# Rows of hx and g at places between the multiples of 32 bytes, and higher feature rates, in a one-core diffusion backbone step

## The chip, the cores and the metric

The kernel runs on one core of one Trainium2 chip. The metric is the device time of one execution in microseconds (us); smaller is better. Engines are named as in the profile: PE is TensorE (matmul), PEld its weight loads, DVE is VectorE, ACT is ScalarE, POOL is GpSimd, SP is SyncE, which issues the DMAs. Every operand of an engine lies in SBUF, 128 partitions wide; a "place" below is a byte address within each partition.

## What is computed

One step of a two-layer transformer for two groups of 128 tokens each (a context prompt and latent tokens), D_MODEL 2048. Both groups go through the same weights, so the kernel puts them side by side: 256 columns. Cut to what matters here:

```python
for l in range(2):
    mod = silu(cond) @ w_ada[l] + b_ada[l]            # six vectors of 2048 for each group
    sh1, sc1, gt1, sh2, sc2, gt2 = split(mod, 6)
    h = rmsnorm(x, g_norm_mix[l]) * (1 + sc1) + sh1   # "modulated"
    x = x + gt1 * mixer(h)                            # layer 0: MLA + GQA, layer 1: differential attention
    h = rmsnorm(x, g_norm_ffn[l]) * (1 + sc2) + sh2   # "modulated"
    u = conv3(h @ w_ffn_up[l])                        # 2048 -> 2 x 5632, then a depthwise convolution
    gate, val = u[..., :5632], u[..., 5632:]
    x = x + gt2 * ((silu(gate) * val) @ w_ffn_down[l])   # "gated"
y = rmsnorm(x, g_final)
```

All inputs and outputs are float32.

## The kernel before, in words

**Precision.** Every large product is made of three matmuls. `split` (L198 to L200) makes of a float32 operand a high part in the type fp32r (a copy by ACT) and the remainder, a low part (a subtraction by DVE). `gemm` (L238 to L248) then adds wh·xh, wh·xl and wl·xh for each block k of 128 input features: L245, L246, L247. The 128x128 block of weights is the loaded operand, the 256 columns of both groups are the moving operand. Weights come by DMA (1 MB each) into `raw` buffers and are split into `wh` and `wl` (`Weights.chunk`).

**Moving operands.** A row of one block k holds 512 numbers in each partition: 256 of the high part, 256 of the low part, 2048 bytes (`ROW` = 512 numbers). `hx` has 16 such rows; it holds the modulated activations (`modulate`, `modulated`, the first one in the main program), and in layer 0 also the attention's output (`o` in `mixer_ab`, under the same tag). `g` is the gated operand of the FFN's down-projection: 22 tiles of one row each (`bufs=KQ`), used twice, since the FFN runs in two halves of 22 blocks (NQ = 2). `oall`, `ql` and `kv_in` are the moving operands of other gemms.

**Places.** Tiles are put at multiples of 32 bytes. `pad` tiles (in `wpool`, `ab`, the FFN's pool and `cc`) move what follows them; SHIFT = 448. With them every row of hx, g, oall, ql and kv_in starts 448 bytes after the start of a weight buffer, modulo 512, which is the length of a 128-column block of weights in a partition. All hx and g rows are at 96, all weight blocks at 160, modulo 512.

**Stages.** Layer 0's mixer (`mixer_ab`, until about 470 us of the span), its FFN (about 490 to 1205), layer 1's mixer (`mixer_c`, to about 1650), the second FFN, and the final norm. An FFN is up(0), down(0), up(1), down(1): `up` has 44 gemms of 16 blocks for each half, `down` 16 gemms of 22 blocks.

**Side work.** The vectors `mod` need 2 x 2048 x 12288 weights (w_ada), which are read beside the gemms. `row_step` does units on PE (L338) or, for a few, on DVE (L367). `feature_step` does one on DVE (L323, one pass over a 128x2048 tile; eight steps make a unit, one DMA feeds two). `pump(rows, feats)`, called after each gemm, adds `feats` to a count and runs one feature step for each whole 1 in it. In the FFN `feats` is FRATE["up"] or FRATE["down"]; it is 0 for the first three blocks of `up` (LATE) and for the last four gemms of the last `down` (QUIET). What is left of the stage's units (13 in the first FFN, 15 by the end of the second: FLIMIT) runs after the last gemm, in the `while` at the end of `ffn`. A scheduler of the framework then orders the instructions of each engine; feature steps keep their order among DVE's pinned ones.

**After a stage.** The next one needs the norm of x: the sums of squares are multiplied out on PE (L179, L180), 1/sqrt on DVE and POOL (L170, L172), spread over partitions (L186 on DVE, L194 on PE), and `modulate` makes the rows of hx, block by block (L434, L440, L443, L444, L446).

Of the kernel before, what the change touches and what calls it, by code (L numbers as in the profile page):

```python
# [17 lines left out]
P = 128  # L18
D = 2048
KD = D // P  # L20
# [2 lines left out]
ROW = 2 * NT  # L23
SHIFT = 448
NL = 2
GRID_W = 64
EPS = 1e-6
MLA_SCALE = (128 + 64) ** -0.5
# [20 lines left out]
    _n += _w  # L49
NCONST = _n  # L50
RATE = {"in": 0.4, "in3": 0.25, "heads": 0.85, "out0": 1.2, "c": 0.65, "outc": 0.65}
FRATE = {"up": 0.735, "down": 1.435}
PEW = {"heads": 1.0, "out0": 1.0, "c": 0.5}
QUIET = [4, 3, 3]
LATE = 3
# [21 lines left out]
def step_kernel(ctx: ExitStack, tc: tile.TileContext, A: dict):  # L77
# [13 lines left out]
    def banks(name):  # L91
        return tc.tile_pool(name=name, bufs=1, space=PSUM)

    uid = [0]

    def nm(s):
# [3 lines left out]
    def T_(pl, shape, tag, dt=F32, bufs=None):  # L100
        kw = {} if bufs is None else {"bufs": bufs}
        return pl.tile(shape, dt, tag=tag, name=nm(tag), **kw)


    T_(wpool, [P, 48], "pad", bufs=1)


    cst = T_(keep, [P, NCONST], "cst")
# [340 lines left out]
    def modulated(st, l, which, units):  # L449
        ensure(l, 3 * which + 1)  # L450
        ensure(l, 3 * which)
        hx = T_(keep, [P, KD, ROW], "hx", F32R)
        modulate(hx, norm_scale(st), l, which, range(KD))
        fill(units)
        return hx
# [73 lines left out]
    def mixer_ab(hx, rb0, st):  # L529
        l = 0  # L530
        with tc.tile_pool(name="ab", bufs=1) as ab:
# [130 lines left out]
            with tc.tile_pool(name="abh", bufs=1) as hp:  # L662
                ada["pew"] = PEW["heads"]

                o = T_(keep, [P, KD, ROW], "hx", F32R)
                load_cw(0)
                WQ = Weights(A["w_q_up"], 6, 2)
                WK = Weights(A["w_kv_up"], 4, 4)
                qh, qlo = (lambda k: ql[:, k, :NT]), (lambda k: ql[:, k, NT:])
                kh, klo = (lambda k: kv_in[:, k, 0]), (lambda k: kv_in[:, k, 1])  # L670
                qn, qr = {}, None

                def gqa_query(h):
                    s2 = T_(tmp, [P, NT], "sq", bufs=2)
                    act.activation(s2, qb[:, h], AF.Square)
                    act.activation(qb[:, h], qb[:, h], AF.Identity, scale=C("gqn"))
                    yield
                    pst = T_(pmisc, [P, 512], "misc")
                    for g in range(2):
                        pe.matmul(pst[:, g:g + 1], s2[:, g * T:(g + 1) * T], inv(128),  # L680
                                  start=True, stop=True)
                    r = rstd(pst[:, 0:2], 2)
                    pool.tensor_scalar(out=rsb[:, h], in0=r[:, 0:2], scalar1=HEAD_SCALE,
                                       scalar2=None, op0=ALU.mult)
                    rope(qb[:, h:h + 1, T:], qb[:, h:h + 1, T:], 1, 64, "rch", "rsh")

                def gqa(h):
                    k = kg[:, h // 4]
                    return head_ab(hp, [(qb[:, h], k)], rsb[:, h], lambda b: vg[:, b, h // 4], o, 8 + h)

                def mla(h, qnh, qrh, knh, vh):
                    half = slice(64 * (h % 2), 64 * (h % 2) + 64)
                    return head_ab(hp, [(qnh, knh), (qrh[half], kr[half])], rsm,
                                   lambda b: vh[:, b], o, h)

                flush()
                start(gqa_query(0))
                for h in range(8):
                    if h % 2 == 0:
                        for i in range(2):  # L700
                            ps = gemm(WQ.chunk(), qh, qlo)
                            qn[h + i] = T_(hp, [P, NT], "qn", bufs=4)
                            act.copy(qn[h + i], ps)
                            pump(RATE["heads"])
                        ps = gemm(WQ.chunk(), qh, qlo)
                        ev = T_(tmp, [P, NT], "nt", bufs=4)
                        act.copy(ev, ps)
                        qr = T_(hp, [P, NT], "qr", bufs=2)
                        act.copy(qr[:, 0:T], ev[:, 0:T])
                        rope(qr[:, None, T:], ev[:, None, T:], 1, 32, "rcm", "rsm")  # L710
                        pump(RATE["heads"])
                    if h < 7:
                        start(gqa_query(h + 1))
                    start(gqa(h))
                    ps = gemm(WK.chunk(), kh, klo, 3 * T)
                    kn = T_(hp, [P, 3 * T], "kn", bufs=2)
                    act.copy(kn, ps)
                    pump(RATE["heads"])
                    ps = gemm(WK.chunk(), kh, klo, 3 * T)
                    vt = T_(hp, [P, 3 * T], "vt", bufs=2)  # L720
                    act.copy(vt, ps)
                    pump(RATE["heads"])

                    def values_and_head(h, vt, *a):
                        pt = T_(ppool["att"], [P, 512], "att", bufs=3)
                        for b in range(3):
                            pe.transpose(pt[:, b * T:(b + 1) * T], vt[:, b * T:(b + 1) * T], ident)
                        vm = T_(hp, [P, 3, P], "vm", bufs=2)
                        act.copy(vm.rearrange("p b d -> p (b d)"), pt[:, :3 * T])
                        yield  # L730
                        yield from mla(h, *a, vm)

                    start(values_and_head(h, vt, qn[h], qr, kn))
                flush()
# [129 lines left out]
    def ffn(hx, l, st):  # L864
        xh, xl = (lambda k: hx[:, k, :NT]), (lambda k: hx[:, k, NT:2 * NT])
        W = Weights(A["w_up"][l], KD, 1)
        WD = Weights(A["w_down"][l], KQ, TB)
        cw = ada["cw"]
        with tc.tile_pool(name=f"ffn{l}", bufs=1) as fp, banks(f"pffn{l}") as pf:
            feat["home"], feat["pool"] = fp, pf  # L870
            T_(fp, [P, SHIFT // 4], "pad")

            def conv(ps, m):
                y = T_(fp, [P, NT], "cv", bufs=3)
                act.activation(y, ps, AF.Identity, scale=cw[:, 1, m:m + 1], bias=cw[:, 3, m:m + 1])  # L875
                y3 = y.rearrange("p (g t) -> p g t", g=2)
                p3 = ps.rearrange("p (g t) -> p g t", g=2)
                dve.scalar_tensor_tensor(out=y3[:, :, 1:], in0=p3[:, :, :T - 1],  # L878
                                         scalar=cw[:, 0, m:m + 1], in1=y3[:, :, 1:],
                                         op0=ALU.mult, op1=ALU.add)  # L880
                dve.scalar_tensor_tensor(out=y3[:, :, :T - 1], in0=p3[:, :, 1:],  # L881
                                         scalar=cw[:, 2, m:m + 1], in1=y3[:, :, :T - 1],
                                         op0=ALU.mult, op1=ALU.add)
                return y

            def up(q):
                gs = []
                for i in range(q * KQ, (q + 1) * KQ):
                    rate = 0 if i < LATE else FRATE["up"]
                    fine[0] = False  # L890
                    gate = conv(gemm(W.chunk(), xh, xl), i)
                    pump(0, rate)
                    if i == 0:
                        load_row()
                    val = conv(gemm(W.chunk(), xh, xl), NFF + i)
                    pump(0, rate)
                    act.activation(gate, gate, AF.Silu)
                    dve.tensor_tensor(out=val, in0=gate, in1=val, op=ALU.mult)
                    g = T_(fp, [P, ROW], "g", F32R, bufs=KQ)
                    split(g[:, :NT], g[:, NT:2 * NT], val)  # L900
                    gs.append(g)
                return gs

            def down(gs, q):
                for c in range(KD):
                    quiet = q == NQ - 1 and c >= KD - QUIET[0]
                    fine[0] = quiet
                    ps = gemm(WD.chunk(), lambda k: gs[k][:, :NT], lambda k: gs[k][:, NT:2 * NT])
                    residual(ps, l, 1, c, st if q == NQ - 1 else None)
                    pump(0, 0 if quiet else FRATE["down"])  # L910

            for q in range(NQ):
                gs = up(q)
                if q == 0:
                    ensure(l, 5)
                down(gs, q)
            while feat["i"] < FLIMIT[stage[0]]:
                feature_step()


    with banks("pab") as ppool["ada"]:
# [5 lines left out]
        st = stat_init()  # L927
        for c in range(KD):
            stat_add(st, x[:, c], KD)
        hx = T_(keep, [P, KD, ROW], "hx", F32R)  # L930
        rb0 = norm_scale(st)
        st = stat_init()
        mixer_ab(hx, rb0, st)
# [150 lines left out]
```

## Time and profile before

| | us |
|---|---|
| Time, median of 3 runs | 2401.15 |
| Lowest, highest | 2400.2, 2407.49 |
| Profiled execution, its time | 2405.92 |
| Profiled execution, its span (first to last instruction) | 2404.2 |
| DVE busy in the span | 1764.9 |
| ACT busy in the span | 1161.7 |
| Moved by DMA | 612.92 MB, 255 GB/s |

How to read it: a page of the profile gives busy times by engine, the granted clock of PE in 40 slices, the chain of work that ended last, and groups of instructions by source line, with the mean duration of one and the idle time before them. A matmul's duration is a latency, because matmuls overlap; its cost in a row of them is the distance between two starts, which the timeline shows.

### The profile page before, as it was taken

Reading aid. Unit: us, or ns where it says so; the run is one execution under the profiler, and the core shown is the slowest. Engines: PE = TensorE matmul, PEld = TensorE weight load, DVE = VectorE, ACT = ScalarE, POOL = GpSimd, SP = SyncE. Lnnn points to the kernel's source line nnn. Section 1 sums busy time; section 2 is a strip of 40 time slices with the busy share of each in tenths; the row PEclk is TensorE's granted clock in tenths of the full one; section 3 lists DMA queues with packets and bytes.
Section 4 is the critical chain, followed back from the end, with each engine's and each line's share of the span. In section 5 each row is a group of like instructions: output and inputs, shape, how many; then the busy total and the mean of one; then the engine's idle time right before and its main releaser. Section 6 shows DMA issues by size and latency. Waiting matters only on the chain.

```text
span 2404.2 us, 47304 instructions
## 1 busy us (share of the span) xinstructions
PE 2329.8 (97%) x19664; PEld 2190.5 (91%) x19664; DVE 1764.9 (73%) x2699; ACT 1161.7 (48%) x1815; POOL 176.3 (7%) x211
## 2 busy tenths in 40 slices
PE   6999999999999999999989999999999999999997
PEld 3778868799999999999969999987999999999997
DVE  2467534579999999999879797876898655666654
ACT  4336544455554355554445454445555534555542
POOL 2002101100000000001210001022000000000011
PEclk9999999999999999999989999999999999999999
DMA  9886678867777877777776777856775555555553
GB/s 394 319 322 245 232 271 311 331 249 266 263 267 284 294 287 263 263 261 278 288 290 230 288 266 275 293 214 249 270 267 198 193 193 193 194 193 193 193 193 123
DMA packets 92549, 612.92 MB, mean 255 GB/s; under 512 B 9968, under 2 KB 17840, under 8 KB 20400
## 3 DMA queue, kind: packets, MB, share of 16 engines
q1 hardware_dynamic: 92336, 609.91, 69.3%
q8 instruction: 154, 2.52, 0.4%
q14 instruction: 59, 0.48, 0.1%
HBM read 605.12 MB, written 4.75 MB: 254 GB/s over the span
## 4 chain that ended last, share of the span: by engine, by line
PE 92%; DMA 4%; DVE 2%; issue 1%; ACT 1%; POOL 0%; POOLq 0%; SPq 0%; DVEq 0%; ACTq 0%
PE acc L245 28%; PE acc L246 28%; PE acc L247 28%; PE ada L338 4%; DMA araw<-w_ada 2%; PE att L509 1%; DMA ckc<-cache_ckv 1%; DMA raw<-w_in_ab 0%; PE ada L286 0%; PE att L801 0%; PE att L499 0%; DMA raw<-w_ada 0%; DMA condb<-condb 0%; DVE nt L440 0%; DVE x L953 0%
## 5 line engine op out<-in xcount | busy, mean ns | idle before, releaser
L199 ACT CAST wh<-raw 128x1024 fp32r<-128x1024 f32 (+1 forms) x788 | 794.4, 1013 | 1007.9 <-PE acc L246 855.7
L200 DVE TENSOR_TENSOR wl<-raw,wh 128x1024 fp32r<-128x1024 f32 (+1 forms) x788 | 921.6, 1182 | 410.3 <-ACT wh L199 402.6
L245 PE MATMUL acc<-hx,wh 128*128 128x256 f32 x4208 | 1170.8, 280 | 12.0 <-ACT hx L444 11.4
L246 PE MATMUL acc<-hx,wh 128*128 128x256 f32 x4208 | 1170.2, 279 | 0.4 <-DVE hx L446 0.4
L247 PE MATMUL acc<-hx,wl 128*128 128x256 f32 x4208 | 1169.0, 278 | 0.0
L245 PEld LDWEIGHTS acc<-hx,wh 128*128 128x128 f32 x4208 | 791.3, 189 | 48.1 <-ACT hx L444 19.4
L246 PEld LDWEIGHTS acc<-hx,wh 128*128 128x128 f32 x4208 | 792.9, 189 | 21.2 <-issue 16.5
L247 PEld LDWEIGHTS acc<-hx,wl 128*128 128x128 f32 x4208 | 792.6, 188 | 13.8 <-issue 13.7
L246 PE MATMUL acc<-g,wh 128*128 128x256 f32 x1408 | 388.3, 276 | 0.0
L247 PE MATMUL acc<-g,wl 128*128 128x256 f32 x1408 | 388.1, 276 | 0.0
L245 PE MATMUL acc<-g,wh 128*128 128x256 f32 x1408 | 387.9, 276 | 0.0
L323 DVE CUSTOM_DVE_ANT_0 junk<-araw,condb 128x2048 f32<-128x2048 f32 x120 | 274.6, 2288 | 0.0
L246 PEld LDWEIGHTS acc<-g,wh 128*128 128x128 f32 x1408 | 264.3, 188 | 0.0
L247 PEld LDWEIGHTS acc<-g,wl 128*128 128x128 f32 x1408 | 264.2, 188 | 0.0
L245 PEld LDWEIGHTS acc<-g,wh 128*128 128x128 f32 x1408 | 264.1, 188 | 0.0
L165 POOL TENSOR_TENSOR sqacc<-sqacc,sq 128x256 f32<-128x256 f32 x76 | 92.9, 1222 | 1530.5 <-issue 1221.2
L338 PE MATMUL ada<-araw,condw 128*32 128x512 f32 x864 | 121.3, 635 | 22.7 <-DMA araw<-w_ada 17.2
L367 DVE SCALAR_TENSOR_TENSOR aacc<-araw,condw,aacc 128x512 f32<-128x512 f32 x150 | 107.7, 747 | 0.3
L875 ACT ACTIVATE cv<-acc,convw 128x256 f32<-128x256 f32 x176 | 98.1, 557 | 0.0
L460 DVE SCALAR_TENSOR_TENSOR x<-acc,mod,x 128x128 f32<-128x128 f32 x192 | 58.1, 344 | 53.4 <-PE acc L247 53.4
L881 DVE SCALAR_TENSOR_TENSOR cv<-acc,convw,cv 128x254 f32<-128x254 f32 x176 | 84.2, 479 | 3.9
L878 DVE SCALAR_TENSOR_TENSOR cv<-acc,convw,cv 128x254 f32<-128x254 f32 x176 | 83.4, 474 | 0.0
(195 smaller groups left out, 1623.3 us busy)
## 6 DMA issues: line engine op xcount, KB each, us to landing
araw<-w_ada SPq DMA_DIRECT2D x188, 1024.0 KB, 5.7
raw<-w_up SPq DMA_DIRECT2D x176, 1024.0 KB, 4.8
raw<-w_down SPq DMA_DIRECT2D x88, 1024.0 KB, 4.8
raw<-w_in_c SPq DMA_DIRECT2D x48, 1024.0 KB, 5.1
raw<-w_in_ab SPq DMA_DIRECT2D x20, 1024.0 KB, 6.9
raw<-w_out_ab SPq DMA_DIRECT2D x16, 1024.0 KB, 6.3
raw<-w_out_c SPq DMA_DIRECT2D x16, 1024.0 KB, 4.9
raw<-w_q_up SPq DMA_DIRECT2D x6, 768.0 KB, 4.6
```

What stands on the lines that cost most here:

```text
L165: pool.tensor_tensor(out=st["acc"], in0=st["acc"], in1=sq, op=ALU.add)
L199: act.copy(out_hi, src)
L200: dve.tensor_tensor(out=out_lo, in0=src, in1=out_hi.bitcast(F32), op=ALU.subtract)
L245: pe.matmul(ps[:, :n], wh, xh(k), start=(i == 0), stop=False)
L246: pe.matmul(ps[:, :n], wh, xl(k), start=False, stop=False)
L247: pe.matmul(ps[:, :n], wl, xh(k), start=False, stop=(i == last))
L323: tc.keep_in_program_order(dve.tensor_tensor_reduce(out=T_(feat["pool"], [P, D], "junk"), in1=feat["row"][:, c], in0=feat["raw"].rearrange ...
L338: i = pe.matmul(ada["ps"][32 * g:32 * g + 32, :], condw[:, 4 * t + g, :], raw[:, g], start=(t == 0), stop=(t == 3), skip_group_check=True)
L367: i = dve.scalar_tensor_tensor(out=acc[:, c], in0=raw[:, g], scalar=condw[:, k, c:c + 1], in1=acc[:, c], op0=ALU.mult, op1=ALU.add)
L875: act.activation(y, ps, AF.Identity, scale=cw[:, 1, m:m + 1], bias=cw[:, 3, m:m + 1])
L878: dve.scalar_tensor_tensor(out=y3[:, :, 1:], in0=p3[:, :, :T - 1], scalar=cw[:, 0, m:m + 1], in1=y3[:, :, 1:], op0=ALU.mult, op1=ALU.add)
L881: dve.scalar_tensor_tensor(out=y3[:, :, :T - 1], in0=p3[:, :, 1:], scalar=cw[:, 2, m:m + 1], in1=y3[:, :, :T - 1], op0=ALU.mult, op1=ALU.add)
```

## The change

Two tables give each row of hx and of g an offset of its own, in numbers of 4 bytes: HX_AT for the 16 rows of hx is 0, 2, 4, 6 by groups of four; G_AT for the 22 rows of g is 4, 4, ... (six times), 6 (six), 9 (five), 11 (five). A small class `Rows` stands for such a tile: `rows[:, k, a:b]` is the slice from ROW * k + at[k] + a. hx grows by 8 numbers (32 bytes), and the pad in `wpool` shrinks by as much, so that the weight buffers stay where they were. g becomes one tile of 22 rows and 16 numbers for each FFN, in place of 22 tiles; it now stands right behind the pad, which is 8 numbers (32 bytes) shorter, and the tiles `cv` and `condb` come after it. oall, ql and kv_in stay.

FRATE goes from 0.735 to 0.75 in `up` and from 1.435 to 1.47 in `down`.

```diff
+
+HX_AT = [2 * (k // 4) for k in range(16)]
+G_AT = [4] * 6 + [6] * 6 + [9] * 5 + [11] * 5
...
-FRATE = {"up": 0.735, "down": 1.435}
+FRATE = {"up": 0.75, "down": 1.47}
...
+    class Rows:
+
+
+        def __init__(self, tile_, at):
+            self.tile_, self.at = tile_, at
+
+        def __getitem__(self, key):
+            _, c, s = key
+            a = ROW * c + self.at[c]
+            return self.tile_[:, a + (s.start or 0):a + s.stop]
...
-    T_(wpool, [P, 48], "pad", bufs=1)
+    T_(wpool, [P, 40], "pad", bufs=1)
...
-        hx = T_(keep, [P, KD, ROW], "hx", F32R)
+        hx = Rows(T_(keep, [P, KD * ROW + 8], "hx", F32R), HX_AT)
         modulate(hx, norm_scale(st), l, which, range(KD))
...
-                o = T_(keep, [P, KD, ROW], "hx", F32R)
+                o = Rows(T_(keep, [P, KD * ROW + 8], "hx", F32R), HX_AT)
...
-            T_(fp, [P, SHIFT // 4], "pad")
+            T_(fp, [P, SHIFT // 4 - 8], "pad")
+            rows = Rows(T_(fp, [P, KQ * ROW + 16], "g", F32R), G_AT)
...
-                    g = T_(fp, [P, ROW], "g", F32R, bufs=KQ)
-                    split(g[:, :NT], g[:, NT:2 * NT], val)
-                    gs.append(g)
+                    k = i - q * KQ
+                    split(rows[:, k, :NT], rows[:, k, NT:2 * NT], val)
+                    gs.append((rows[:, k, :NT], rows[:, k, NT:2 * NT]))
...
-                    ps = gemm(WD.chunk(), lambda k: gs[k][:, :NT], lambda k: gs[k][:, NT:2 * NT])
+                    ps = gemm(WD.chunk(), lambda k: gs[k][0], lambda k: gs[k][1])
...
-        hx = T_(keep, [P, KD, ROW], "hx", F32R)
+        hx = Rows(T_(keep, [P, KD * ROW + 8], "hx", F32R), HX_AT)
         rb0 = norm_scale(st)
```

## The prediction

> **What bounds the kernel now.** I read the page first, engines and slices, then the chain of waits.
>
> ```profile
> span 2404.2 us, 47304 instructions
> PE 2329.8 (97%) x19664; PEld 2190.5 (91%) x19664; DVE 1764.9 (73%) x2699; ACT 1161.7 (48%) x1815; POOL 176.3 (7%) x211
> PEclk9999999999999999999989999999999999999999
> PE 92%; DMA 4%; DVE 2%; issue 1%; ACT 1%; POOL 0%; POOLq 0%; SPq 0%; DVEq 0%; ACTq 0%
> ```
>
> TensorE (PE) is busy 97% of the span at full granted clock, and 92% of the chain that ended last is PE. So the time is a count of matmuls times what one of them takes, plus some stops at the stage borders. Next the groups of instructions, for the counts:
>
> ```profile
> L245 PE MATMUL acc<-hx,wh 128*128 128x256 f32 x4208 | 1170.8, 280 | 12.0 <-ACT hx L444 11.4
> L246 PE MATMUL acc<-hx,wh 128*128 128x256 f32 x4208 | 1170.2, 279 | 0.4 <-DVE hx L446 0.4
> L247 PE MATMUL acc<-hx,wl 128*128 128x256 f32 x4208 | 1169.0, 278 | 0.0
> L245 PE MATMUL acc<-g,wh 128*128 128x256 f32 x1408 | 387.9, 276 | 0.0
> L286 PE MATMUL ada<-cst,am 128*128 128x128 f32 x122 | 19.4, 279 | 4.4 <-ACT am L280 4.4
> ```
>
> 3 x 4208 = 12,624 matmuls stream rows of hx and 3 x 1408 = 4,224 rows of g. Their mean of 276 to 280 ns is a latency, since matmuls overlap; what one costs is the distance from start to start. That is read from the timeline. The first two rows are six matmuls apart, the next two eighteen; the last is four matmuls of 128 columns in one row.
>
> ```profile
> 699.80 0.28 PE L247 MATMUL acc<-hx,wl 128*128 128x256 f32 x1
> 700.48 0.28 PE L247 MATMUL acc<-hx,wl 128*128 128x256 f32 x1
> ...
> 1579.81 0.28 PE L246 MATMUL acc<-oall,wh 128*128 128x256 f32 x1
> 1581.93 0.28 PE L246 MATMUL acc<-oall,wh 128*128 128x256 f32 x1
> ...
> 1237.49 0.60 PE L286 MATMUL ada<-cst,am 128*128 128x128 f32 x4
> ```
>
> 0.68 / 6 = 113.3 ns, and 2.12 / 18 = 117.8 ns: two rhythms of one instruction form, with the same weight load and the same distance (448 bytes modulo 512) between moving row and weight buffer. The fast one is the rule:
>
> ```profile
> 600.00:900.00 300.00, 300.00 (x2650) 300.00 (x2649) 280.00 (x347) 142.43 (x177) 0.00 (x0) 1.00 0.76 278
> 1045.00:1160.00 115.00, 115.00 (x1017) 115.00 (x1016) 109.59 (x127) 53.87 (x68) 16.20 (x8) 1.00 0.77 279
> 1595.00:1640.00 45.00, 45.00 (x384) 45.00 (x384) 24.73 (x37) 19.54 (x31) 10.24 (x8) 1.00 0.53 188
> 1880.00:1990.00 110.00, 110.00 (x973) 110.00 (x972) 64.37 (x83) 47.35 (x54) 0.00 (x0) 1.00 0.55 192
> ```
>
> These windows (length; then busy time and count of PE, weight loads, DVE, ACT, POOL; clock; DMA) lie in the first ConvFFN, twice, in the output projection of layer 1, and in the second ConvFFN. 300 / 2650 = 113.2 ns in the first row, 113.1 in the second and the last, whether DVE is at 95% (109.59 of 115) or at 59%, and DMA at 0.77 or 0.55. The third has 117.2, with less beside it than any other. So in 113.3 ns there is no wait for another engine: it is what the array and its two streams of operands do by themselves. A lower bound for the pair of weight load and matmul comes from the L286 row: four matmuls, each with a 128x128 load, take 0.60 us, less one latency of 279 ns: 107 ns. So at most about 6 ns of each 113 is an extra that depends on something else.
>
> [...]
>
> **The change, part by part.**
>
> *Places.* HX_AT puts rows 0 to 3 of hx where they were, and rows 4 to 7, 8 to 11, 12 to 15 at 8, 16, 24 bytes further. G_AT is 16, 24, 36, 44 bytes, and the pad ahead of g is 32 bytes shorter: so g's rows move by -16 (six rows), -8 (six), +4 (five), +12 bytes (five). Pads keep every weight buffer, and oall, ql and kv_in, where they were. No instruction is added or removed: 12,624 x 3/4 = 9,468 matmuls on hx and all 4,224 on g, 13,692 in all, read from another place. What that is worth no row shows directly, since every gemm of this trace has the one distance. So I bound it.
> Best: each moved matmul falls to the 107 of L286: 13,692 x 6.3 ns = 86 us. Worst that a row shows: each goes to the other rhythm: 13,692 x 4.5 = 62 us more.
> My value: 1,024 bytes of a row go by in 113.3 ns, so 8 bytes are 0.89 ns. [...] I let each move take its own length off the extra. hx: moves of 0, 8, 16, 24 bytes, mean 12, 1.33 ns x 12,624 = 16.8 us. g: (6x16 + 6x8 + 5x4 + 5x12) / 22 = 10.2 bytes, 1.13 ns x 4,224 = 4.8 us. Together 21.6 us, a quarter of the best case, since all moves lie within 28 bytes of a 512-byte distance. That the sign is a gain is the weakest step; it is weighed below.
>
> *Writers.* ACT and DVE write these rows in instructions of 0.4 us; they are under PE in the FFN, and on the chain only at the start of a stage. If the places cost each of them what 16 bytes of 1,024 are, 6 ns, 16 rows x 3 stages x 2 writers come to 0.6 us. I take nothing.
> *g as one tile.* Before, 22 buffers were reused by the second half of the FFN; now 22 slices are. Each write waits for the reads of its own slice, as before: nothing.
>
> *Rates.* In the first FFN 104 feature steps are due. pump counts 0.735 on 82 calls and 1.435 on 28: 60.3 + 40.2 = 100.5, so 100 run inside and 4 after the last gemm. With 0.75 and 1.47 it is 61.5 + 41.2 = 102.7: 102 inside, 2 after. What the four do now, by DVE's timeline, then PE's:
>
> ```profile
> 1205.88 2.29 DVE L323 CUSTOM_DVE_ANT_0 junk<-araw,condb 128x2048 f32<-128x2048 f32 x1
> 1209.22 0.15 DVE L170 TENSOR_SCALAR rv<-misc 128x2 f32<-128x2 f32 x1
> 1209.29 2.29 DVE L323 CUSTOM_DVE_ANT_0 junk<-araw,condb 128x2048 f32<-128x2048 f32 x1
> 1212.17 0.48 DVE L186 TENSOR_SCALAR diag<-cst,rr 128x128 f32<-128x128 f32 x2 [0.53 <-POOL rr L172]
> 1212.56 2.29 DVE L323 CUSTOM_DVE_ANT_0 junk<-araw,condb 128x2048 f32<-128x2048 f32 x1
> 1214.78 1.41 DVE L434 TENSOR_TENSOR nt<-x,misc 128x256 f32<-128x256 f32 x4
> 1216.10 2.29 DVE L323 CUSTOM_DVE_ANT_0 junk<-araw,condb 128x2048 f32<-128x2048 f32 x1
> 1218.31 1.11 DVE L440 TENSOR_SCALAR nt<-nt,scl,mod 128x128 f32<-128x128 f32 x4
> ...
> 1212.80 1.19 PE L194 MATMUL misc<-diag,cst 128*128 128x256 f32 x2 [4.98 <-DVE diag L186]
> 1218.51 1.94 PE L338 MATMUL ada<-araw,condw 128*32 128x512 f32 x8 [4.52 <-DVE mod L323]
> 1220.37 0.80 PE L245 MATMUL acc<-hx,wh 128*128 128x256 f32 x2
> ```
>
> The third and the fourth step stand in the way of the norm that the first gemm of layer 1 waits for. In the changed order they are the two that leave. Without the third, L434 can begin when L194 ends (1212.80 + 1.19 = 1213.99 instead of 1214.78): 0.8 us. Without the fourth, L440 follows L434 directly: 2.2 us. Gain 3.0 us; at most 4.6 (two steps of 2.29), at least 0, if the row steps L338 are what is late next. The two steps go under PE into the first FFN, whose tightest window above leaves DVE 115 - 109.59 = 5.4 us; were that cover gone they would cost their 4.6 us. One more 1 MB load there meets DMA at 0.77. In the second FFN the 16 steps only end sooner.
>
> *Sum.* The profiled execution took 2405.9 us, 1.7 beside its span. 2405.9 - 21.6 - 3.0 = 2381.3. It lies 4.8 us over the median of the runs (2401.15), so the median goes to about 2377.
>
> **The rivals.**
> (a) *The places do nothing.* For it: the rhythm is the same for hx and g, and with busy and idle neighbours, as a fixed cost would be. Against it: 117.8 at the same places shows a cost that isn't fixed. Only the tail is left: 2401.2 - 3.0 = 2398. [...]
> (b) *A row that starts inside a 16-byte piece touches one piece more, and the result is slower.* A row of 1,024 bytes is 64 pieces of 16; at a start off that grid it touches 65. Rows at +8 and +24 of hx (half of 12,624) and at -8, +4, +12 of g (16 of 22 of 4,224) are such: 6,312 + 3,072 = 9,384 matmuls x 113.3 / 64 = 1.77 ns: 16.6 us, less 3.0: 2415. It decides where the extra piece isn't hidden in the 6 ns over L286; nothing in this trace starts off that grid, so no row speaks against it. [...]
> (c) *The moves push gemms into the slow rhythm.* 117.8 exists, and holds for whole stretches, as in the 45 us window of the output projection; that stage follows attention, whose short matmuls cut into the gemms. A jump of place three times in each gemm might do the same. In full 62 us, less 3: 2460; with half of the rows 2429. Against it: hx and g keep the fast rhythm through both FFNs undisturbed.
> [...]
>
> **How the numbers follow.** A measurement here can't tell less than about 0.3%, 7 us, from no change. Forecast 0.48; (a) 0.15; (b) 0.17; (c) 0.15; (d) 0.05. I put the forecast ahead of (b) and (c) because g's moves go to both sides of the old place and all four groups differ: what costs at one place is then bounded by the others, while the fast rhythm that holds across every neighbour's load speaks against (c). The forecast alone reaches from 2350 (twice the value) to 2392 (a third of it). To leave out no more than 2 in 10, the range takes in (a), (b) and the half of (c), and below all but the end of (d): 2341 to 2430. Faster by over 0.3%: the forecast and (d), less the forecast's small end: 0.50. Within 0.3%: (a) and that end: 0.17. Slower: (b), (c): 0.33.
>
> **What would show it.** Start-to-start distances of the hx and g matmuls: near 112 ns in the FFN windows, about 2,680 matmuls in 300 us instead of 2,650, and steps by group of rows in the timeline. Rows of oall stay at 117.8 or 113.3. The first gemm of layer 1 follows L194 by about 4.6 us instead of 7.6, with two L323 steps between the last L460 and L434 instead of three, and none after it. Wrong if the distance is still 113.3 (a), if the rows at +8 and +24 alone are longer (b), if long stretches of an FFN run at 117 and over (c), or if PE gets idle time behind wl in the first FFN, since then DVE has become the bound.

## The result, and the profile after

| | before | after |
|---|---|---|
| Time, median, us | 2402.2 (4 runs) | 2486.3 (4 runs) |
| Ratio of after to before, 95% interval | | 1.0338, 1.0322 to 1.0354 |
| Span of the profiled execution, us | 2404.2 | 2479.8 |

The change makes the kernel 3.4% slower; the prediction had 2377 us and a range of 2341 to 2430. The page of the profile after, in the lines that were read before:

```profile
span 2479.8 us, 47330 instructions
PE 2411.2 (97%) x19664; PEld 2272.5 (92%) x19664; DVE 1764.2 (71%) x2699; ACT 1157.3 (47%) x1815; POOL 168.1 (7%) x211
PE 94%; DMA 3%; DVE 1%; issue 1%; ACT 1%; POOL 0%; SPq 0%; POOLq 0%; DVEq 0%; ACTq 0%
L259 PE MATMUL acc<-hx,wh 128*128 128x256 f32 x4208 | 1192.2, 285 | 11.4 <-ACT hx L458 10.5
L259 PE MATMUL acc<-g,wh 128*128 128x256 f32 x1408 | 396.7, 282 | 0.0
```

PE is busy 81 us longer with the same 19,664 matmuls; DVE and ACT have the same work in the same time; PE still hardly waits (11.4 us in front of 4,208 matmuls of L259, where it was 12.0 at L245, the same line of the code). So no new wait: the matmuls themselves take longer. The windows show it. Rows of PE alone (length; busy time and count; clock; DMA share; GB/s), first of before, then of after; the first of each pair is an `up` stretch, that is hx alone, the second a `down` stretch, g alone. A count holds two matmuls that began ahead of the window. Only the moving rows of hx and g, which lie in SBUF like the weights, have new places; the sums `acc` are in PSUM and did not move.

```profile
920.00:1020.00 100.00, 100.00 (x885) 1.00 0.74 269
2002.00:2024.00 22.00, 22.00 (x197) 1.00 0.56 194
```

```profile
920.00:1020.00 100.00, 100.00 (x846) 1.00 0.70 259
2002.00:2024.00 22.00, 22.00 (x186) 1.00 0.51 176
```

100 / 883 = 113.3 ns has become 100 / 844 = 118.5 on hx, and 22 / 195 = 112.8 has become 22 / 184 = 119.6 on g; the clock is 1.00 in all four. Added up over all starts of the two traces, matmuls on hx take 1477.1 us before and 1533.7 after (+56.6), on g 478.7 and 504.8 (+26.1), on oall, which was not moved, 94.5 and 91.3 (-3.2), everything else on PE 3.6 less. The sum is 75.9 us, against 75.6 between the two spans.

Which rows pay is seen inside one gemm. Below are single starts of a gemm of `up` in the trace after: of its matmuls number 0, 4, 12, 24, 36, and number 0 of the next gemm. Three matmuls belong to a row, so 12, 24 and 36 are the first ones at +8, +16 and +24 bytes.

```profile
903.61 0.28 PE L259 MATMUL acc<-hx,wh 128*128 128x256 f32 x1
904.08 0.28 PE L260 MATMUL acc<-hx,wh 128*128 128x256 f32 x1
904.99 0.28 PE L259 MATMUL acc<-hx,wh 128*128 128x256 f32 x1
906.43 0.28 PE L259 MATMUL acc<-hx,wh 128*128 128x256 f32 x1
907.86 0.28 PE L259 MATMUL acc<-hx,wh 128*128 128x256 f32 x1
909.30 0.28 PE L259 MATMUL acc<-hx,wh 128*128 128x256 f32 x1
```

From 4 to 12, in the rows that stayed: 0.91 / 8 = 114 ns. At +8: 1.44 / 12 = 120; at +16: 1.43 / 12 = 119; at +24: 1.44 / 12 = 120. Even the rows that stayed pay once: their first four matmuls, after the last rows of the gemm before, take 0.47 / 4 = 118. So each group of moved rows is slower than the rows at the old place in this gemm, and the slowdown ends within four matmuls when the place is the old one again.

The means over the distances between two starts of the same group of rows, interruptions over 128 ns left out, in ns:

```
bytes moved        -16    -8     0     +4    +8   +12   +16   +24
hx (after)                      115.2        120.1       118.9  120.4
g  (after)        118.9  119.7        121.4        118.1
```

### The profile page after: what moved, and what is told of

It reads as the page before. It is cut to its first block, busy times and chain, and to the rows that moved or that the text cites. A ratio compares the mean times of both kernels' runs of the same rounds, so it can differ in the third digit from the quotient of the medians.

```text
span 2479.8 us, 47330 instructions
## 1 busy us (share of the span) xinstructions
PE 2411.2 (97%) x19664; PEld 2272.5 (92%) x19664; DVE 1764.2 (71%) x2699; ACT 1157.3 (47%) x1815; POOL 168.1 (7%) x211
## 4 chain that ended last, share of the span: by engine, by line
PE 94%; DMA 3%; DVE 1%; issue 1%; ACT 1%; POOL 0%; SPq 0%; POOLq 0%; DVEq 0%; ACTq 0%
PE acc L259 29%; PE acc L261 29%; PE acc L260 29%; PE ada L352 4%; DMA araw<-w_ada 1%; PE att L523 1%; DMA ckc<-cache_ckv 1%; PE ada L300 0%; DMA raw<-w_in_ab 0%; PE att L815 0%; DMA raw<-w_ada 0%; PE att L513 0%; DMA condb<-condb 0%; DVE x L968 0%; PE ada L287 0%
## 5 line engine op out<-in xcount | busy, mean ns | idle before, releaser
L259 PE MATMUL acc<-hx,wh 128*128 128x256 f32 x4208 | 1192.2, 285 | 11.4 <-ACT hx L458 10.5
L260 PE MATMUL acc<-hx,wh 128*128 128x256 f32 x4208 | 1189.5, 283 | 0.0
L261 PE MATMUL acc<-hx,wl 128*128 128x256 f32 x4208 | 1188.5, 283 | 0.0
L259 PEld LDWEIGHTS acc<-hx,wh 128*128 128x128 f32 x4208 | 797.0, 190 | 50.2 <-ACT hx L458 19.1
L261 PEld LDWEIGHTS acc<-hx,wl 128*128 128x128 f32 x4208 | 800.7, 190 | 13.0 <-issue 12.9
L259 PE MATMUL acc<-g,wh 128*128 128x256 f32 x1408 | 396.7, 282 | 0.0
L260 PE MATMUL acc<-g,wh 128*128 128x256 f32 x1408 | 396.5, 282 | 0.0
L261 PE MATMUL acc<-g,wl 128*128 128x256 f32 x1408 | 396.4, 282 | 0.0
L259 PEld LDWEIGHTS acc<-g,wh 128*128 128x128 f32 x1408 | 265.4, 189 | 0.0
L474 DVE SCALAR_TENSOR_TENSOR x<-acc,mod,x 128x128 f32<-128x128 f32 x192 | 58.3, 345 | 57.7 <-PE acc L261 57.6
```

Of the source, the lines that this page charges most:

```text
L259: pe.matmul(ps[:, :n], wh, xh(k), start=(i == 0), stop=False)
L260: pe.matmul(ps[:, :n], wh, xl(k), start=False, stop=False)
L261: pe.matmul(ps[:, :n], wl, xh(k), start=False, stop=(i == last))
```

## The experiments

All are made from the kernels before and after. "Distance" is the start of the moving row less the start of the weight block, modulo 512 bytes. All means in this part are over the starts of a whole stretch of the trace: for hx the second half's `up` of the first FFN, for g the first `down` of the second FFN. Before, both are 113.33.

**The two parts of the change, each alone.**

```diff
-FRATE = {"up": 0.735, "down": 1.435}
+FRATE = {"up": 0.75, "down": 1.47}     # e1_rates
+FRATE = {"up": 0.765, "down": 1.5}     # e2_no_left
```

> The rates alone, all places as before. Theory (places cost the time): start-to-start distances stay 113.3 ns in both FFNs; two feature steps instead of four after the first FFN, and the time is 1 to 3 us under the kernel before. Rival (the higher rates are what costs, DVE or DMA falling behind in the first FFN): tens of us over it, with idle PE in the first FFN.

> Rates 0.765 and 1.5: 62.7 + 42.0 = 104.7, so all 104 steps run inside the first FFN and none is left. Theory: 2 to 5 us under the kernel before, since the norm's chain has DVE for itself. Rival (DVE, busy 109.6 of 115 us in the tightest stretch, falls behind): PE idles in the first FFN and the time is the same or longer than with 0.75 and 1.47.

Measured: with the change's rates 0.9981 of before (0.9971 to 0.9991), with the higher ones 0.9974 (0.9962 to 0.9985); hx and g at 113.33 in both. By the medians that is 3.7 and 7.6 us, more than the 1 to 3 and the 2 to 5 expected. So the rates are no part of the loss. Both kernels are a little faster than the one before, but their intervals overlap, so which of the two rates is better stays open. The norm between the first FFN and layer 1, by the timeline, first with the change's rates, then with none left over:

```profile
1206.21 0.61 DVE L460 SCALAR_TENSOR_TENSOR x<-acc,mod,x 128x128 f32<-128x128 f32 x2 [0.48 <-PE acc L247]
1210.15 2.29 DVE L323 CUSTOM_DVE_ANT_0 junk<-araw,condb 128x2048 f32<-128x2048 f32 x1
1210.31 2.68 POOL L172 TENSOR_TENSOR rr<-rv,cst 128x2 f32<-128x2 f32 x1 [9.25 <-DVE rv L170]
1217.90 1.06 PE L338 MATMUL ada<-araw,condw 128*32 128x512 f32 x8 [2.27 <-DMA araw<-w_ada]
1218.90 0.50 PE L245 MATMUL acc<-hx,wh 128*128 128x256 f32 x2
```

```profile
1206.71 0.61 DVE L460 SCALAR_TENSOR_TENSOR x<-acc,mod,x 128x128 f32<-128x128 f32 x2 [0.60 <-PE acc L247]
1209.68 0.70 POOL L172 TENSOR_TENSOR rr<-rv,cst 128x2 f32<-128x2 f32 x1 [8.34 <-DVE rv L170]
1216.10 0.80 PE L245 MATMUL acc<-hx,wh 128*128 128x256 f32 x2
```

From the last residual (L460) to the first gemm: 1218.90 - 1206.21 = 12.7 us and 1216.10 - 1206.71 = 9.4 us. Before it was 1220.37 - 1205.36 = 15.0, with POOL as slow as in the first of the two:

```profile
1205.36 0.61 DVE L460 SCALAR_TENSOR_TENSOR x<-acc,mod,x 128x128 f32<-128x128 f32 x2 [0.48 <-PE acc L247]
1209.45 2.68 POOL L172 TENSOR_TENSOR rr<-rv,cst 128x2 f32<-128x2 f32 x1 [9.25 <-DVE rv L170]
```

```diff
-HX_AT = [2 * (k // 4) for k in range(16)]
-G_AT = [4] * 6 + [6] * 6 + [9] * 5 + [11] * 5
+HX_AT = [0] * 16                          # e3_no_move; e4_hx_groups keeps HX_AT
+G_AT = [8] * 22                           # both: g where it was before
```

> The changed code (hx and g read through Rows, g as one tile) with all offsets so chosen that each row lies where it lay before; rates as before. Theory: 113.3 ns everywhere, time of the kernel before within 0.2%. Rival (one tile for g brings waits or another order): slower by some tenths of a per cent, with distances of 113.3 but idle PE.

> Only hx gets its four groups of places, g lies as before, rates as before. Theory (each operand pays for its own places): g stays at 113.3 ns, hx at about 119, the time 54 to 58 us over the kernel before. Rival (an interplay, one operand's places upset the other's gemms): g leaves 113.3 too.

Measured: without a move 1.0002 (0.9993 to 1.0011), 113.33 for both operands. The new code with the old places is the old kernel. With hx alone moved 1.0246 (1.0232 to 1.0260), hx 118.6, g 113.35; 2463.8 is 59.5 us over 2404.3, a little more than the 54 to 58 expected. Each operand pays for its own places. The windows of that run:

```profile
920.00:1020.00 100.00, 100.00 (x845) 1.00 0.69 253
2002.00:2024.00 22.00, 22.00 (x197) 1.00 0.58 194
```

**Steps between groups, the distance, or the grid?** From here on every kernel ran once. Runs of the kernel before lie between 2400.2 and 2408.4 us, so times that differ by 40 us and more are clear of that, and 6 to 8 us are not. Three explanations were left: the jumps of place within a gemm; the distance from the weights; or a start off a multiple of some number of bytes. First no jumps:

```diff
+HX_AT = [2] * 16      # e5_flat_8_16: hx +8 bytes, distance 456
+G_AT = [12] * 22      #               g +16 bytes, distance 464
+HX_AT = [8] * 16      # e6_flat_32_64: hx +32, distance 480
+G_AT = [24] * 22      #                g +64, distance 0
```

> No groups: all hx rows 8 bytes further, all g rows 16 bytes further, weights as before. Theory 'grid' (a moving row that starts off a multiple of 32 bytes is slow, wherever): hx about 120 ns, g about 119 ns, time about 2400 + 12,624 x 6.5 ns + 4,224 x 5.5 ns = 2505 us. Theory 'distance' (448 bytes modulo 512 from the weights is the good distance, any other is worse): the same. Rival 'jumps' (the steps of place between the groups are what costs): both 113.3 ns, 2400 us.

> No groups: all hx rows 32 bytes further, all g rows 64 bytes further; so all on the grid of 32, at distances 480 and 0 instead of 448. Grid: 113.3 ns for both, time that of the kernel before. Distance: hx above 113.3, by the growth from +8 to +24 (120 ns) about 120 to 125, g other again, time over 2470 us.

Measured: 2505.7 us, hx 120.0, g 119.2; and 2485.1 us, hx 118.3, g 120.0. "Jumps" falls with the first run, "grid alone" with the second. Their windows, in this order:

```profile
920.00:1020.00 100.00, 100.00 (x835) 1.00 0.68 246
2002.00:2024.00 22.00, 22.00 (x187) 1.00 0.51 182
```

```profile
920.00:1020.00 100.00, 100.00 (x847) 1.00 0.70 258
2002.00:2024.00 22.00, 22.00 (x186) 1.00 0.54 191
```

Then the weights are moved. They are put into one tile and handed out by turns, so that they too can start between the tiles' multiples of 32:

```diff
+    W_AT = 2
+    wall = T_(wpool, [P, 8 * 1024 + 8], "wall", F32R, bufs=1)
...
-                        wh_ = T_(wpool, [P, 1024], "wh", F32R, bufs=4)
-                        wl_ = T_(wpool, [P, 1024], "wl", F32R, bufs=4)
+                        a = W_AT + 1024 * (wslot[0] % 4)
+                        wslot[0] += 1
+                        wh_, wl_ = wall[:, a:a + 1024], wall[:, a + 4096:a + 5120]
```

> hx and g rows and all weight buffers 8 bytes further: off the grid of 32, at the old distance of 448. Grid: hx and g at about 120 ns, time about 2500 us. Distance: hx and g at 113.3 ns, and only oall, ql and kv_in (now at 440) slower, which is 1,176 matmuls and at most 8 us.

> Only the weight buffers 8 bytes further; all moving rows on the grid of 32, distance 440. Grid, for moving rows alone: 113.3 ns, time that of the kernel before. Grid, for both operands: slower, as in the run with both moved or less. Distance: about 120 ns, as -8 bytes of g showed, time about 2510 us.

Measured: 2566.7 us, hx 120.0; and 2533.7 us, hx 118.3. In these two some weight blocks of the down projections are overwritten before they are read, so they do not compute the same step, and in their g stretches PE also waits; only hx is read from them. "Distance alone" falls: at 448, with both operands 8 bytes further, hx is at 120. It was repeated with a mended order (a buffer's second half is split only when needed), beside a control and two moves by 32:

> Again hx, g and all weight buffers 8 bytes further (distance 448, off the grid of 32), now with weights split into halves of a buffer only when they are needed, so that none is overwritten before it is read. Theory 'both' (the fast rhythm needs the distance 448 and a start on the grid of 32): about 120 ns for hx and g, as in the first run of these places, 2490 to 2520 us. Rival 'distance alone': 113.3 ns and about 2400 us, and the first run was slow by its overwritten blocks.

> hx, g and all weight buffers 32 bytes further: distance 448, on the grid, at other absolute places (128 and 192 instead of 96 and 160, modulo 512). Theory 'both': 113.3 ns for hx and g, 2400 to 2410 us. Rival 'absolute place' (only 96 beside 160 is good): 117 to 120 ns, over 2460 us.

> Control for the two above: weight buffers as slices of one tile, split in halves when needed, all places as before. Every theory: 113.3 ns; 2400 to 2410 us, or more by what the later splits cost in idle PE.

> Only the weight buffers 32 bytes further, rows as before: on the grid, distance 416 (the other side of 448 than the run with hx at +32). Theory 'both': slower than 113.3 ns, about 118 as at 480, time about 2470 to 2490 us. Rival 'grid alone with an exception at 480 and 0': 113.3 ns and 2400 us.

Measured: both +8, 2524.3 us, hx 120.7, g 120.1 (120.0 in other stretches of that trace). Both +32, 2410.9 us, 113.33 for both operands. Control, 2411.5 us, 113.33 for both (8 us over before; g in the first FFN had a stretch at 117.8, which cost 4 us, and the later splits may cost the rest). Weights +32 alone, 2491.6 us, 118.7 for both. The two slow times are 4 and 2 us over what was expected. So distance 448 is good at two absolute places if the starts are on the grid, and bad off it; other distances are bad on the grid. The two windows of the run with both +8, then of the run with both +32, then of the run with the weights alone at +32:

```profile
920.00:1020.00 100.00, 100.00 (x830) 1.00 0.68 247
2002.00:2024.00 22.00, 22.00 (x185) 1.00 0.54 186
```

```profile
920.00:1020.00 100.00, 100.00 (x885) 1.00 0.73 268
2002.00:2024.00 22.00, 22.00 (x197) 1.00 0.56 200
```

```profile
920.00:1020.00 100.00, 100.00 (x845) 1.00 0.69 253
2002.00:2024.00 22.00, 22.00 (x187) 1.00 0.52 180
```

**Which grid, and does the distance repeat?** In the first run HX_AT, G_AT and W_AT add 16 bytes to everything; in the second hx goes 128 and g 256 bytes further.

> hx, g and all weight buffers 16 bytes further, distance 448. Theory 'grid of 32': about 120 ns for hx and g, about 2500 us. Rival 'grid of 16' (a start on a multiple of 16 is enough, so that the +16 and -16 groups of the change paid for their distance only): 113.3 ns, 2405 to 2412 us.

> Weights as before; all hx rows 128 bytes further (distance 64), all g rows 256 bytes further (distance 192), all on the grid of 32. Theory 'one good distance in 512': both over 113.3 ns, 117 to 125 ns, over 2470 us. Rival 'the good distances repeat every 128 or 256 bytes': both at 113.3 ns (128), or g alone (256).

Measured: both +16, 2410.6 us, 113.33 for both operands, where both +8 had 120.7 and 120.1: the grid is 16 bytes, not 32. Far moves, 2449.6 us: hx at distance 64 runs at 117.78 in all four `up` stretches, g at distance 192 at 113.34. So the good distance repeats after 256 bytes. After 128 it does not in the FFNs, but distance 64 is not like the other bad ones: in layer 1's mixer of the same trace hx at this distance also runs at 113.3 for some 14 us at a time. The windows of the two runs, with one from that mixer as the last row:

```profile
920.00:1020.00 100.00, 100.00 (x885) 1.00 0.73 269
2002.00:2024.00 22.00, 22.00 (x197) 1.00 0.57 200
```

```profile
920.00:1020.00 100.00, 100.00 (x851) 1.00 0.70 255
2002.00:2024.00 22.00, 22.00 (x196) 1.00 0.56 193
1537.00:1548.00 11.00, 11.00 (x99) 1.00 0.76 292
```

11 / 97 = 113.4 ns in that row. Over any 24 starts in a row, the operands at distances 0, 160, 176, 208 and 224 have no mean under 117.

The steady rhythms side by side, ns from start to start, in the FFNs; for oall, in layer 1's output projection:

| run | operand | distance mod 256 | both starts on 16 bytes | ns |
|---|---|---|---|---|
| before | hx, g | 192 | yes | 113.33 |
| both +16, both +32 | hx, g | 192 | yes | 113.33 |
| far | g | 192 | yes | 113.34 |
| both +8 | hx, g | 192 | no | 120.7, 120.1 |
| weights +32 | hx, g | 160 | yes | 118.7 |
| flat +16 | g | 208 | yes | 119.2 |
| flat +32 | hx | 224 | yes | 118.3 |
| flat +64 | g | 0 | yes | 120.0 |
| both +16 (the oall rows did not move) | oall | 176 | yes | 118.7 |
| far | hx | 64 | yes | 117.8 (113.3 in parts of layer 1's mixer) |
| flat +8 | hx | 200 | no | 120.0 |
| weights +8 | hx | 184 | no | 118.3 |

## Why the prediction was wrong

- **What bounds the kernel: right.** The loss of 76 us in the span is matmul rhythm, 83 us on hx and g less 7 elsewhere; no wait for another engine or DMA came into it. The prediction read the 113.3 ns as what PE's two streams of operands do by themselves, and the runs bear that out: with the same engines beside it, moving one of the streams, or both, by 8 bytes changes it on hx: 113.33 becomes 120.0 (rows), 118.3 (weights) and 120.7 (both).
- **The places: wrong, in sign and size.** The step that failed is "I let each move take its own length off the extra": it took the extra over the 107 ns of L286 as something a small move lessens, 21.6 us in all. That was the author's estimate; no run shows a matmul that loses a move's length, 0.89 ns for 8 bytes. Measured in the trace after: +4.5 ns on hx as a mean over its 12,624 matmuls (1533.7 - 1477.1 us) and +6.2 on g (504.8 - 478.7), 83 us more. No run of the study has a steady rhythm under 113.3, so that the extra can be lessened at all is not shown. The 107 was misread too: single starts of L286 in the trace before are 109 ns apart (65 of 88 distances), and they move 128 columns, not 256, so they are no floor that these matmuls were seen to reach. The two rhythms, 113.3 and 117.8, occur at the same places, so they had said that the rhythm can change, not that a place sets it, nor that the old place was anything but the best.
- **The argument for the sign: wrong.** "What costs at one place is then bounded by the others" treats good and bad places as two sides of a slope. They are not: of the distances tried on the 16-byte grid only 192 modulo 256 gives 113.3, and its neighbours on that grid on either side (160, 176, 208, 224) give 118 to 119 (64 has both rhythms, see below). The groups leave the good distance in both directions.
- **Rival (a)**, no effect: fell. In the windows above PE is busy all the time (100.00 of 100 us, 22.00 of 22), so no other engine keeps it waiting there, and yet its rhythm is 113.33 or 118.7 ns by the distance of its two operands alone (control against weights +32).
- **Rival (b)**, the 16-byte grid: right as to the grid, too small in price and incomplete. Rows and weights 8 bytes off it cost 7 ns, not 1.77, at the good distance (both +8 against both +16), and the groups at +16 and -16, which it left free, cost nearly as much by their distance (118.9 ns, hx at +16 and g at -16 in the trace after). With both operands moved alike it is 113.33 at +16 and 120.7 and 120.1 at +8. The two prices do not add: off the grid and off the distance (flat +8) is 120.0 too.
- **Rival (c)**, the slow rhythm: nearest to what came, by another mechanism. It had 62 us for all moved rows at 117.8; it was 83, since moved rows take 118 to 121 and the rows that stayed pay after each jump back. But jumps between groups are not what does it: flat places are as slow (2505.7 us, slower than the change, because there all hx rows are moved). The chance of 0.15 and the cut at half of it made the range too short.
- **Rival (d)**, which the range takes in down to 2341: nothing like it. The lowest steady rhythm that any run has on hx and g is 113.33 ns.
- **Writers and one tile for g: right**, nothing (no move: 1.0002).
- **Rates: right in sign, the tail's gain too large.** The tail shrank by 15.0 - 12.7 = 2.3 us where 3.0 was predicted, in the trace after by 1.3 (1260.01 - 1246.34 = 13.7, by the two rows below, where L474 and L259 are what L460 and L245 were). The ratio 0.9981 with its interval is a gain of 2 to 7 us. The prediction had named what could lessen it: a row step on PE (L338, 1217.90 + 1.06 in the rows above) ends just where the first gemm starts; in the trace after the same step takes 1.94 us. How much of the difference it is was not tried. The steps moved into the first FFN are hidden, as costed.

```profile
1246.34 0.61 DVE L474 SCALAR_TENSOR_TENSOR x<-acc,mod,x 128x128 f32<-128x128 f32 x2 [0.63 <-PE acc L261]
1260.01 0.80 PE L259 MATMUL acc<-hx,wh 128*128 128x256 f32 x2
```

- **Two slips that changed nothing.** The window with the slow rhythm has not "less beside it than any other": POOL is busiest there (10.24 of 45 us). POOL is not the cause, since without a move the same window has the same 10.24 us and runs at 113.3. And 0.17 + 0.15 is 0.32, not 0.33.

## What to carry to other kernels

In these traces the weight loads run beside the matmuls (PE and PEld are both busy for 300.00 of 300 us), and where the two operands lie, to each other and on the grid, was worth 4 to 6.5% of the rhythm (113.33 ns against 117.8 to 120.7): read the distance from start to start in a stretch where PE waits for nobody, by row if rows lie differently, before and after any change of layout. A place that a kernel's pads hold at an odd-looking number (448) is to be taken as a narrow optimum until a trace shows a neighbour (here 113.33 ns at 448, 118.7 and 118.3 at 32 bytes to either side); and one run with all rows moved alike shows the price of a place more plainly than four places at once. Work left over at the end of a stage is best kept out of the next stage's norm: with none in it, the norm here took 9.4 us in place of 15.0.

## What the runs showed that was not expected

- In the FFNs, but for the two stretches of g named below, the rhythm goes by the distance of the two starts modulo 256 bytes and by a 16-byte grid, and not by the absolute place: 113.33 at three pairs of absolute places and at two distances 256 apart. Why is not settled: the runs show when it happens, not what inside TensorE or the memory makes it. Of the 16 distances on that grid seven were tried, so a better one is not excluded.
- A slow rhythm of 117.8 also occurs at the good place: in the trace before on oall through most of layer 1's output projection, in the trace after not (113.3 there, 3.2 us gained), with the same places. So the 3.2 us are no gain of the change; the run without a move has 113.3 there too. The traces show where the rhythm changes: at an interruption, after which it stays. In the control (weights in one tile, no move) two starts of g that come 0.24 and 0.23 us after the ones before, at 1104 us, are followed by 117.8 to the end of the FFN; the two rows of PE below are from ahead of them and behind them (100 / 849 = 117.8). In the run with the rates 0.765 and 1.5, one start of g that comes 0.17 us after the one before, at 1170 us, is followed by the same. At distance 64 it goes the other way: behind some interruptions in the mixer hx runs at 113.3 until the next interruption, while in the FFN it drops to 117.8 at once behind g's 113.3, with no interruption. So at 192 and at 64 both rhythms hold, and which one a stretch gets depends also on what ran before it; what in the interruption decides was not tried.

```profile
1087.00:1103.00 16.00, 16.00 (x144) 1.00 0.65 248
1107.00:1207.00 100.00, 100.00 (x851) 1.00 0.76 281
```

- POOL's power of 2 numbers per partition (L172) took 2.68 us beside a feature step on DVE and 0.70 us without one, in the rows above. POOL's instruction starts 0.16 us after the feature step and ends 0.55 us after it (1210.31 + 2.68 against 1210.15 + 2.29), and by the same times in the trace before (1209.45 + 2.68 against 1209.29 + 2.29). What makes it long there is not shown. Its 2.0 us (2.68 - 0.70) may be part of the 5.6 us that the norm gains without any step in it (15.0 - 9.4).
